# Sums of the weights of the last stages made early and kept in DRAM, and rows of x added by transfers

## The chip, the core and the metric

The kernel runs on one core of a Trainium2 chip. The metric is device time in microseconds (us) of one execution; the time before is the median of three runs. A core has five engines with one instruction queue each, and they meet only through semaphores: TensorE (PE, with its weight loads as PEld), VectorE (DVE), ScalarE (ACT), GpSimd (POOL) and SyncE (SP). In this kernel SP and POOL issue the DMA transfers. An engine takes its instructions strictly in order, so one that waits holds back everything behind it.

## The reference

x is 1024 tokens by 1024 channels, in float32. One block is computed:

```
h = rms_norm(x, norm_g);  proj = h @ w_in            # u, g_rnn, q, k, v, g_attn, m_rnn, m_attn
y_rnn  = rg_lru(conv(u)) * silu(g_rnn)               # a recurrence along the tokens
y_attn = sliding_window_attention(q, k, v) * silu(g_attn)
merged = sigmoid(m_rnn) * (y_rnn @ w_rnn_out) + sigmoid(m_attn) * (y_attn @ w_attn_out)
out = rms_norm(x + merged @ w_o, final_norm_g)
```

## The kernel before

**Products.** Every large matrix product is done by a scheme with seven block products in place of eight. A unit takes 256 output channels. Its weights are four blocks A11, A12, A21, A22 (128 partitions by 512), its right side is four block rows B11, B12, B21, B22 of four tiles each. The scheme multiplies A11 by B11, A12 by B21, A22 by T4, and the sums S1 = A21 + A22, S2 = S1 - A11, S3 = A11 - A21, S4 = A12 - S2 by T1, T2, T3 and B22, where T1 to T4 are differences of the B blocks. Each factor is cut into a high and a low part (names ending in h and l): ACT makes the high one by a cast (L430), DVE the low one by a subtraction (L431). Each block product is then three matmuls per tile (L510 to L512), so a unit is 7 x 4 x 3 = 84 matmuls.

**Stages.** After the norm of x and its transposes come 24 units of the input projection (two more are done directly, at the start): ug (recurrence branch and its gate, followed by `lru` on DVE and ACT), k, v, q, ga (attention gate), mr and ma (merge gates). Between them stand 32 attention units a00 to a37. Then come eight units for the two output projections: zr0 to zr3 on y_rnn, and za0 to za3 on y_attn. Their results are multiplied by the merge gates (tile tz, L1034). The zr results stay in SBUF as MG, and the za results are added to them, which gives `merged`. Last is the product with w_o (matmuls L1162 to L1164, PSUM tiles named o): the four blocks of MG are the A side, split into mh and ml, and w_o the B side. Its first product is A11 by B11, its second S1 by T1. From the seven products come u2, u3 and c1, to which rows of x are added on DVE, and then the norm of each row tile (`row_out`, L1182) and the store.

**Where the weights come from.** The A blocks are loaded by POOL (L421) into a class of buffers named raw; the table TUNE gives it 5 buffers. The sums S1 to S4 are made on DVE (L438) just before they are split, for the z units too. For w_o the differences T1 to T4 are made on DVE in `comb_from`.

**What sets the order.** The program first lists all operations with their reads and writes. `Plan.run` then places them one by one on the engines, by its own costs, by a priority for each operation and by the numbers in TUNE (caps of buffer classes, priorities, and `orders`, the sequence of units). That placement becomes the instruction order of each queue. So every number in TUNE can move instructions anywhere in the program; an operation with no early inputs missing may be placed far ahead of where `orders` names it.

## Time and profile before

| | |
|---|---|
| median of 3 runs (lowest to highest) | 896.63 us (896.55 to 897.25) |
| the profiled execution's own time | 896.38 us |
| its span in the profile | 894.5 us |
| PE busy | 862.4 us, 96% of the span |
| DVE busy | 772.0 us, 86% |
| ACT busy | 633.0 us, 71% |
| moved by DMA | 129.77 MB, mean 145 GB/s |

The span starts with the first instruction and ends with the last; the profiled execution's own time has 1.9 us more around it. PE is the engine to look at, since its work cannot be spread to others; wherever PE waits, the profile names the instruction that released it. Stages can be told apart by time: the first unit's products start at 47.3 us, its last evicted block is added at 91.2 us, the z units run from 653 to 805.3 us, the product with w_o from 805.3 to 886.1 us, and what follows is the end of the last rows.

### The profile page before, as it was taken

Reading aid. Unit: us, or ns where it says so; the run is one execution under the profiler, and the core shown is the slowest. Engines: PE = TensorE matmul, PEld = TensorE weight load, DVE = VectorE, ACT = ScalarE, POOL = GpSimd, SP = SyncE. Lnnn points to the kernel's source line nnn. Section 1 sums busy time; section 2 is a strip of 40 time slices with the busy share of each in tenths; the row PEclk is TensorE's granted clock in tenths of the full one; section 3 lists DMA queues with packets and bytes.
Section 4 is the critical chain, followed back from the end, with each engine's and each line's share of the span. In section 5 each row is a group of like instructions: output and inputs, shape, how many; then the busy total and the mean of one; then the engine's idle time right before and its main releaser. Section 6 shows DMA issues by size and latency. Waiting matters only on the chain.

```text
span 894.5 us, 13047 instructions
## 1 busy us (share of the span) xinstructions
PE 862.4 (96%) x4040; PEld 711.5 (80%) x4040; DVE 772.0 (86%) x1571; ACT 633.0 (71%) x1326; POOL 73.0 (8%) x131
## 2 busy tenths in 40 slices
PE   4999999999999999999999999999999989998996
PEld 3778888888777788887888887888888878877885
DVE  6995778799999858888787977677999899999998
ACT  7654485889999558786998999979874445344631
POOL 2100000000010100001001000000100100000000
PEclk9999999999999999999999999999999999999998
DMA  9314626112236675677524645353765570493005
GB/s 321 122 42 130 159 83 206 53 34 73 77 86 175 214 209 148 166 195 212 160 77 119 193 113 165 119 168 114 219 199 177 182 253 24 164 317 119 0 1 212
DMA packets 86886, 129.77 MB, mean 145 GB/s; under 512 B 10656, under 2 KB 40224, under 8 KB 86816
## 3 DMA queue, kind: packets, MB, share of 16 engines
q1 hardware_dynamic: 77216, 97.47, 35.1%
q0 software_dynamic: 9600, 31.46, 12.2%
q8 instruction: 32, 0.52, 0.2%
q14 instruction: 38, 0.31, 0.1%
HBM read 87.21 MB, written 41.68 MB: 144 GB/s over the span
## 4 chain that ended last, share of the span: by engine, by line
PE 62%; DVE 24%; ACT 8%; issue 4%; DMA 2%; SPq 0%; DVEq 0%; ACTq 0%
PE pair L510 17%; PE pair L511 16%; PE pair L512 16%; PE ps_s L901 3%; DVE cu L731 2%; PE ptp L935 2%; DVE hs L764 2%; DVE wl L431 2%; ACT sm L916 2%; DVE ml L431 2%; DVE S L438 2%; DVE c L438 1%; ACT sm L924 1%; PE fd L568 1%; PE fd L567 1%
## 5 line engine op out<-in xcount | busy, mean ns | idle before, releaser
L421 POOL DMA_DIRECT2D A<-in_wall_dram x120 | 64.6, 539 | 681.9 <-PE po L949 111.5
L430 ACT CAST wh<-S 128x512 fp32r<-128x512 f32 x128 | 78.6, 620 | 18.7 <-PE pair L512 7.8
L431 DVE TENSOR_TENSOR wl<-S,wh 128x512 fp32r<-128x512 f32 x128 | 87.0, 683 | 5.3 <-ACT wh L430 4.1
L431 DVE TENSOR_TENSOR wl<-A,wh 128x512 fp32r<-128x512 f32 x96 | 65.5, 683 | 4.7 <-ACT wh L430 3.1
L430 ACT CAST wh<-A 128x512 fp32r<-128x512 f32 x96 | 59.4, 619 | 7.6 <-PE pair L511 2.8
L916 ACT ACTIVATE sm<-sm,nm 128x256 f32<-128x256 f32 (+1 forms) x128 | 62.0, 488 | 1.0 <-DVE nm L909 0.9
L909 DVE CUSTOM_DVE_ANT_0 sm<-ps_s,mask_t,sink_t 128x256 f32<-128x256 f32 (+1 forms) x128 | 54.0, 459 | 3.4 <-PE ps_s L901 3.1
L924 ACT ACTIVATE sm<-sm,dn 128x256 f32<-128x256 f32 (+1 forms) x128 | 53.5, 489 | 2.5 <-DVE dn L921 2.4
L510 PE MATMUL pair<-T3h,wh 128*128 128x512 f32 x128 | 50.5, 395 | 1.3 <-ACT u L526 1.3
L510 PE MATMUL pair<-B11h,wh 128*128 128x512 f32 x128 | 51.2, 400 | 0.5 <-DVE B12l L427 0.5
L510 PE MATMUL pair<-T4h,wh 128*128 128x512 f32 x128 | 50.9, 397 | 0.8 <-ACT u L533 0.7
L511 PE MATMUL pair<-T2l,wh 128*128 128x512 f32 x128 | 50.0, 391 | 1.6 <-DVE T2l L431 1.6
L510 PE MATMUL pair<-T2h,wh 128*128 128x512 f32 x128 | 51.4, 401 | 0.2 <-ACT c L523 0.2
L438 DVE TENSOR_TENSOR c<-pair,u 128x512 f32<-128x512 f32 x64 | 43.8, 684 | 8.8 <-ACT u L533 4.6
L510 PE MATMUL pair<-T1h,wh 128*128 128x512 f32 x128 | 51.3, 401 | 0.0
L512 PE MATMUL pair<-B11h,wl 128*128 128x512 f32 x128 | 50.1, 391 | 1.0 <-DVE wl L431 1.0
L510 PE MATMUL pair<-B22h,wh 128*128 128x512 f32 x128 | 49.9, 390 | 0.7 <-DVE c L438 0.7
L510 PE MATMUL pair<-B21h,wh 128*128 128x512 f32 x128 | 50.6, 395 | 0.0
L512 PE MATMUL pair<-T4h,wl 128*128 128x512 f32 x128 | 50.0, 390 | 0.0
L511 PE MATMUL pair<-T3l,wh 128*128 128x512 f32 x128 | 50.0, 390 | 0.0
L512 PE MATMUL pair<-T2h,wl 128*128 128x512 f32 x128 | 50.0, 390 | 0.0
L511 PE MATMUL pair<-B22l,wh 128*128 128x512 f32 x128 | 49.9, 390 | 0.0
(270 smaller groups left out, 2588.7 us busy)
## 6 DMA issues: line engine op xcount, KB each, us to landing
A<-in_wall_dram POOLq DMA_DIRECT2D x120, 256.0 KB, 3.3
qt<-st_q SPq DMA_DIRECT2D x32, 256.0 KB, 3.9
xt<-in_x_dram SPq DMA_DIRECT2D x16, 256.0 KB, 5.4
A<-in_wall_dram SPq DMA_DIRECT2D x16, 256.0 KB, 4.9
tm_r<-tm SPq DMA_DIRECT2D x16, 256.0 KB, 2.5
K<-st_k SPq DMA_DIRECT2D x32, 128.0 KB, 3.1
yr_dr<-tg SPq DMA_DIRECT2D x16, 256.0 KB, 2.2
st_q<-qh SPq DMA_DIRECT2D x32, 128.0 KB, 2.5
```

Source lines behind the costliest of these rows:

```text
L421: pl.op([("POOL", 1000.0)], reads, writes, lambda e: nc.gpsimd.dma_start(dst(), src()), prio, move=move)
L430: ACT(lambda e: e.copy(h(), src()), cols, reads, wh, prio)
L431: (DVE if psum else EW)(lambda e: e.tensor_tensor(l(), src(), h().bitcast(F32), op=ALU.subtract), cols, list(reads) + list(wh), wl, prio)
L438: (eng or EW)(lambda e: e.tensor_tensor(dst.t, a.t, b.t, op=op), HF, [a, b], [dst], prio)
L510: nc.tensor.matmul(ps.t, h.t[:, w], bh.t, start=start and k == 0, stop=False, **kw)
L511: nc.tensor.matmul(ps.t, h.t[:, w], bl.t, start=False, stop=False, **kw)
L512: nc.tensor.matmul(ps.t, l.t[:, w], bh.t, start=False, stop=k == 3, **kw)
L731: DVE(lambda v, j=j, w=w, cu=cu, u=u: v.scalar_tensor_tensor(cu.t[:, j:], u.t[:, : HF - j], w(), cu.t[:, j:], op0=MUL, op1=ADD), HF, [u, c ...
L901: nc.tensor.matmul(ps.t[:, j, o0 : o0 + pw], qt.t[:, h, :], K[m, half].t[:, c0 : c0 + pw], start=m == 0, stop=m == 1)
L909: DVE(lambda v, ps=ps, j=j, h=h, s=s: v.tensor_tensor_reduce(s.t[:, j, :], ps.t[:, j, :], att["mask"].t[:, 256 - w : 256], scale=-0.125, s ...
L916: ACT(lambda e, h=h, s=s, j=j: e.activation(s.t[:, j, :], s.t[:, j, :], AF.Exp, scale=-1.0, bias=nm.t[:, h : h + 1], accum_out=dn.t[:, h : ...
L924: ACT(lambda e, h=h, s=s, j=j: e.activation(s.t[:, j, :], s.t[:, j, :], AF.Identity, scale=dn.t[:, h : h + 1]), w, [(s, j), dn], [(s, j)], ...
```

## The change

1. **Sums kept in DRAM.** A new function `sums(j)` loads the four blocks of a z unit again through a small buffer class sr (issued by SP), makes S1 to S4 on DVE and stores them to a DRAM tensor. Then the z unit loads S1 to S4 (through POOL, into the raw buffers) and makes no sums; it also needs no A21. `orders` names s0, s1, s3, s4, s5, s6 (units zr0, zr1, zr3, za0, za1, za2) and s10. zr2 and za3 still make their sums in place. s10 makes T1 to T4 for one quarter of w_o, but the loads of such T tiles are only built if table 8 exists, and it does not: the four tiles of s10 are made and stored and never read.
2. **Merged part in DRAM** (`mgd` 1): the zr results are stored to DRAM (16 stores) and loaded again (tile mg, 16 loads) when the za results are added.
3. **x added by transfers** (`xacc` 1): twelve of the sixteen row tiles of x are added to u3, u2 and c1 by adding transfers, which POOL issues (`ADDTO`), in place of 12 loads on SP and 12 adds on DVE.
4. **Numbers.** Nearly all numbers in TUNE and the sequence of units are others; the raw class has 4 buffers now, for A blocks and loaded sums together.

```diff
 TUNE = {
-    'm': (29, 3, 3),
+    'm': (30, 3, 3),
...
-    'raw': 5,
-    'raws': 9,
-    'S': 5,
+    'raw': 4,
+    'raws': 10,
+    'S': 6,
...
-    'gt': -5,
+    'gt': -4,
...
+    'sump': 200,
+    'sumq': 0,
+    'sr': 5,
+    'srs': 8,
+    'xacc': 1,
+    'macc': 0,
     'lo': 0,
-    'mgd': 0,
-    'orders': 'k0 ug0 v0 ug5 ug3 ug6 ug7 ug2 ug4 q0 a00 ga0 q1 ma0 a01 a02 a03 a10 q2 a11 a04 a12 q3 '
-              'ma1 a13 a05 a14 a06 a07 a15 ug1 a20 a21 mr2 ga1 a16 a17 a22 a23 a24 a25 ga3 a26 a30 '
-              'a31 a32 ga2 ma3 a33 a34 a35 a36 a27 mr3 a37 ma2 zr0 zr1 zr2 zr3 za0 za1 za2 za3',
+    'mgd': 1,
+    'orders': 'ug0 k0 ug7 v0 ug5 ug4 ug3 ug1 q0 q1 ug2 a00 ga0 ma2 a01 a02 a03 a10 a11 a04 a05 q3 a12 '
+              'a13 ga3 a14 q2 a15 s0 a06 s5 a07 s10 ug6 s3 ma1 mr3 a16 a20 a21 a17 s4 s6 a22 a23 a24 '
+              'ma0 ga2 a25 s1 a26 a30 a31 a32 a33 a34 ma3 a35 a36 a27 mr2 ga1 a37 zr0 zr1 zr2 zr3 za0 '
+              'za1 za2 za3',
...
+    def ADDTO(dst, src, nbytes, reads, writes, prio=0):
+
+        pl.op([("POOL", 1000.0)], list(reads) + list(writes), writes, lambda e: nc.gpsimd.dma_start(dst(), src(), accum_op=ADD),
+              prio, move=2 * nbytes / 16 / 2048 * 84)
...
+            if j in sum_dr:
+                if name not in A:
+                    t, m = buf(self.cls, name=name), int(name[1]) - 1
+                    A[name] = t
+                    DMA(lambda: t.t, lambda: sum_dr[j][m], 1 << 18, [(sum_dr[j], m)], [t], self.prio, by=self.by)
+                return A[name]
...
+    def sums(j):
...
+        d = sum_dr[j] = dr.tile([4, P, HF], F32, name=f"sum{j}")
+        T = {}
+
+        def raw(n, ap):
+            T[n] = load("sr", "sr")
+            DMA(lambda: T[n].t, ap, 1 << 18, [], [T[n]], TUNE["sump"], by="POOL" if TUNE["sumq"] else "SP")
+
+        def make(m, n, a, b, op):
+            t = T[n] = buf("ss", name=n)
+            tt(t, T[a], T[b], op, TUNE["sump"])
+            DMA(lambda: d[m], lambda: t.t, 1 << 18, [t], [(d, m)], TUNE["sump"])
...
+                   {n: [((lambda m=m, k=k: sum_dr[8 + k][m]), [(sum_dr[8 + k], m)]) for k in range(4)]
+                    for m, n in enumerate(("T1", "T2", "T3", "T4")) if 8 in sum_dr})
...
+    def plus_x(t, r, c):
+
+        if TUNE["xacc"]:
+            ADDTO(lambda: t.t, lambda: x[r * P : (r + 1) * P, HALF[c]], 1 << 18, [], [t], TUNE["xof"])
+            return t
+        y = x_rows(r, c)
+        tt(y, y, t, ADD)
+        return y
...
     for i in range(4):
-        XO[i + 4, 1] = x_rows(i + 4, 1)
         tt(u3[i], d[i], u3[i], ADD, 0, DVE)
-        tt(XO[i + 4, 1], XO[i + 4, 1], u3[i], ADD)
+        XO[i + 4, 1] = plus_x(u3[i], i + 4, 1)
```

How the change moves instructions is shown at three places. The first is DVE in the first 45 us, between the splits of the first unit and T1, the first difference of the second half of x. Before, the four sums there belong to a unit that soon runs:

```order
L431 TENSOR_TENSOR wl_537<-S3_497,wh_530 128x512
L703 TENSOR_SCALAR acc_95<-acc_95 128x8
L704 TENSOR_TENSOR acc_95<-acc_95,zz_255 128x8
L706 SCALAR_TENSOR_TENSOR acc_95<-acc_95,ab_126 128x8
L707 TENSOR_SCALAR sp4_547<-acc_95 128x8
L708 TENSOR_SCALAR nsp8_549<-acc_95 128x8
L438 TENSOR_TENSOR S1_554<-A21_499,A22_501 128x512
L438 TENSOR_TENSOR S2_559<-S1_554,A11_267 128x512
L438 TENSOR_TENSOR S3_564<-A11_267,A21_499 128x512
L438 TENSOR_TENSOR S4_568<-A12_528,S2_559 128x512
L668 SCALAR_TENSOR_TENSOR T1_590<-pt_573,vec_t_99,F11_292 128x512
```

And now they are five of the sums that will be kept (their inputs are sr):

```order
L443 TENSOR_TENSOR wl_565<-S3_516,wh_556 128x512
L725 TENSOR_TENSOR acc_102<-acc_102,zz_262 128x8
L450 TENSOR_TENSOR S2_573<-S1_546,sr_288 128x512
L727 SCALAR_TENSOR_TENSOR acc_102<-acc_102,ab_133 128x8
L450 TENSOR_TENSOR S3_579<-sr_288,sr_274 128x512
L728 TENSOR_SCALAR sp4_589<-acc_102 128x8
L729 TENSOR_SCALAR nsp8_591<-acc_102 128x8
L450 TENSOR_TENSOR S4_594<-sr_293,S2_573 128x512
L450 TENSOR_TENSOR S1_611<-sr_299,sr_548 128x512
L689 SCALAR_TENSOR_TENSOR T1_625<-pt_601,vec_t_106,F11_307 128x512
```

The sums of the next unit moved behind the T splits, and the kept sums begin here. All 28 of them stand in DVE's order ahead of the end of the third unit's recurrence work (the last, S4_1535, stands beside the first operations of the second `lru`), so they are made before any attention unit, not where `orders` names them.

The second place is POOL's queue at the start of the zr units. Before it holds only A blocks:

```order
L421 DMA A11_7148<-in_wall_dram 128x512
L421 DMA A21_7210<-in_wall_dram 128x512
L421 DMA A22_7280<-in_wall_dram 128x512
L421 DMA A12_7422<-in_wall_dram 128x512
L421 DMA A11_7505<-in_wall_dram 128x512
```

Now each unit that has kept sums loads seven tiles (sum0 belongs to zr0):

```order
L428 DMA A11_7069<-in_wall_dram 128x512
L428 DMA S1_7122<-sum0_93 128x512
L428 DMA S2_7255<-sum0_93 128x512
L428 DMA A12_7329<-in_wall_dram 128x512
L428 DMA S3_7393<-sum0_93 128x512
L428 DMA A22_7441<-in_wall_dram 128x512
L428 DMA S4_7474<-sum0_93 128x512
L428 DMA A11_7533<-in_wall_dram 128x512
```

Four loads in a unit became seven, through four buffers in place of five.

The third place is DVE where the last z unit ends and the product with w_o begins. ml is the low part of a block of MG, and the product A11 by B11 needs four of them. Before, three (ml_9128, ml_9135, ml_9142) stand 13 operations further ahead, and the fourth, ml_9210, behind the gate work of the last unit (c12_9166 is its last block):

```order
L1034 SCALAR_TENSOR_TENSOR tz_9178<-tz_9178,c12_9166 128x512
L438 TENSOR_TENSOR tz_8283<-tz_8283,tz_9178 128x512
L1034 SCALAR_TENSOR_TENSOR tz_9189<-tz_9189,pair_8849 128x512
L438 TENSOR_TENSOR tz_8289<-tz_8289,tz_9189 128x512
L1034 SCALAR_TENSOR_TENSOR tz_9196<-tz_9196,c22_9084 128x512
L438 TENSOR_TENSOR tz_8294<-tz_8294,tz_9196 128x512
L431 TENSOR_TENSOR ml_9210<-tz_8010,mh_9144 128x512
L438 TENSOR_TENSOR S1_9212<-tz_7863,tz_8161 128x512
```

Now the last two of the four, ml_9257 and ml_9266, stand ahead of it, with S1's first tile right behind them:

```order
L450 TENSOR_TENSOR mg_9184<-mg_9184,tz_9178 128x512
L443 TENSOR_TENSOR ml_9257<-mg_8670,mh_9242 128x512
L443 TENSOR_TENSOR ml_9266<-mg_8690,mh_9259 128x512
L450 TENSOR_TENSOR c22_9268<-pair_9119,u3_9261 128x512
L443 TENSOR_TENSOR T1l_9274<-T1_9065,T1h_9237 128x512
L450 TENSOR_TENSOR S1_9281<-mg_8564,mg_9184 128x512
```

The split that the first w_o product waits for moved from behind 13 operations to ahead of them. On PE, nine matmuls of that product now stand before the last two block products of za3, and the other 39 after them.

More of the change, by code (lines that the diff above doesn't have):

```diff
@@ L36 @@
     'pen': 99999,
-    'zy': 7,
-    'zg': 2,
-    'raw': 5,
-    'raws': 9,
-    'S': 5,
+    'zy': 5,
+    'zg': 3,
+    'raw': 4,
+    'raws': 10,
+    'S': 6,
     'wc': 11,
     'B': 11,
-    'psw': 92,
-    'psk': 0,
-    'Y': 10,
-    'ld': 9,
-    'lds': 25,
+    'psw': 58,
+    'psk': 1,
+    'Y': 9,
+    'ld': 14,
+    'lds': 21,
     'kv': 8,
-    'kvs': 4,
+    'kvs': 3,
     'qt': 3,
-    'qts': 3,
-    'P': 17,
+    'qts': 5,
+    'P': 16,
     'AO': 22,
-    'AOs': 18,
+    'AOs': 17,
     'xo': 24,
-    'lru0': -183,
+    'lru0': -135,
     'xos': 10,
-    'prep': 244,
+    'prep': 270,
     'att': 91,
     'val': 95,
-    'gate': 893,
-    'lru': -1188,
-    'qk': -306,
-    'comb': 349,
-    'ztl': 300,
-    'xof': 497,
-    'gzr': 14,
-    'gza': 44,
+    'gate': 951,
+    'lru': -1407,
+    'qk': -125,
+    'comb': 348,
+    'ztl': -10,
+    'xof': 233,
+    'gzr': 8,
+    'gza': 42,
     'gwo': 14,
     'gxo': 3,
-    'gt': -5,
+    'gt': -4,
     'seven': 'ra',
@@ L484, in left @@
                 return raw(name)
+            j = self.i - U_ZR if self.i < U_K else 4 + self.i - U_ZA
+            if self.i not in range(U_ZR, U_K) and self.i < U_ZA:
+                j = -1
+            if j in sum_dr:
[4 more added lines that the diff above has]
+                return A[name]
             src = A[name] = buf("S", name=name)
@@ L992, in whole_from, with comb_from @@
         return get
-    def comb_from(src, after, prio):
+    def comb_from(src, after, prio, more={}):
         C, Y, T = {}, {}, {}
@@ L1008, in right @@
                 return raw(n)
+            if n not in T and n in more:
+                T[n] = [load("Y", n) for _ in range(4)]
+                for k in range(4):
+                    DMA(lambda k=k: T[n][k].t, more[n][k][0], 1 << 18, more[n][k][1] + after, [T[n][k]], prio)
             if n not in T:
@@ L1076, in hybrid_block_kernel @@
     for w in TUNE["orders"].split():
[L1077 removed]
+        seq.append(("a", int(w[1]), int(w[2])) if w[0] == "a" else ("s", int(w[1:])) if w[0] == "s" else (w[:-1], int(w[-1])))
     base = {"ug": U_UG, "mr": U_MR, "k": U_K, "v": U_V, "q": U_Q, "ma": U_MA, "ga": U_GA, "zr": U_ZR, "za": U_ZA}
[L1079 removed]
+    ids = [base[a] + p for a, p in (it for it in seq if len(it) == 2 and it[0] != "s")]
     POS.update({u: i for i, u in enumerate(ids)})
@@ L1123, in hybrid_block_kernel @@
     for it in seq:
+        if it[0] == "s":
+            sums(it[1])
+            continue
         if len(it) == 2:
@@ L1222, in hybrid_block_kernel @@
     for i in range(4):
-        tt(XO[i, 0], b[i], c1[i], ADD, 0, DVE)
+        tt(XO[i, 0], b[i], XO[i, 0], ADD, 0, DVE)
         row_out(i, [XO[i, 0], XO[i, 1]])
```

35 lines of the change are left out of this document (26 added, 9 removed).

## The prediction

> **What bounds the kernel now.** I read the engine table first, then the busy time by stage, then the waits of PE, then the timeline at the longest late wait.
>
> ```profile
> PE 862.4 (96%) x4040; PEld 711.5 (80%) x4040; DVE 772.0 (86%) x1571; ACT 633.0 (71%) x1326; POOL 73.0 (8%) x131
> ```
>
> The change touches no matmul, so PE's work stays and only its 894.5 - 862.4 = 32.1 us without work, and time at a lower clock, can go. Where they lie is in the table of stretches (columns: stretch in us and its length; busy us and instructions of PE, PEld, DVE, ACT, POOL; granted clock, DMA share, GB/s). The stretches are the start, the first unit, units with VectorE free, units with VectorE full, attention, the z units, the first product with w_o, its other six, and the end. The last two rows, from a second table, are the two z units in which PE waits.
>
> ```profile
> 7.90:47.30 39.40, 33.81 (x161) 27.25 (x161) 36.18 (x97) 29.99 (x64) 8.32 (x6) 0.96 0.60 215
> 47.30:91.20 43.90, 43.56 (x191) 35.71 (x192) 33.44 (x54) 20.38 (x38) 2.69 (x5) 1.00 0.32 86
> 91.20:186.00 94.80, 94.80 (x427) 78.20 (x426) 74.77 (x127) 64.99 (x109) 8.05 (x15) 1.00 0.41 122
> 186.00:281.00 95.00, 93.36 (x408) 75.93 (x408) 93.35 (x151) 88.14 (x138) 9.67 (x18) 1.00 0.26 77
> 281.00:653.00 372.00, 369.19 (x1870) 308.47 (x1870) 299.67 (x735) 315.17 (x765) 32.24 (x60) 1.00 0.58 165
> 653.00:805.30 152.30, 149.07 (x654) 121.98 (x654) 148.28 (x244) 73.30 (x134) 11.28 (x21) 1.00 0.55 184
> 805.30:820.20 14.90, 12.66 (x48) 9.65 (x47) 14.59 (x25) 3.83 (x9) 0.00 (x0) 0.90 0.49 172
> 820.20:886.10 65.90, 65.89 (x290) 54.20 (x288) 64.98 (x124) 32.20 (x65) 0.00 (x0) 1.00 0.14 49
> 886.10:894.50 8.40, 0.00 (x0) 0.00 (x0) 4.70 (x12) 0.59 (x2) 0.00 (x0) 0.66 0.51 187
> ...
> 729.00:748.00 19.00, 16.44 (x71) 12.84 (x70) 19.00 (x33) 10.63 (x20) 1.87 (x4) 1.00 0.16 53
> 786.00:805.30 19.30, 18.62 (x83) 15.09 (x82) 19.08 (x32) 9.41 (x18) 0.00 (x0) 1.00 0.91 321
> ```
>
> Three things are to be seen. From 653 us on VectorE is as full as PE (148.28 of 152.3 us, then 14.59 of 14.9), and here PE waits: 19.00 - 16.44 = 2.56 us in the first za unit, 19.30 - 18.62 = 0.68 in the last. From 186 to 281 us VectorE is full too (93.35 of 95), and PE loses 1.64. From 47.3 to 186 us VectorE is free for 43.90 - 33.44 + 94.80 - 74.77 = 30.5 us. The waits name VectorE:
>
> ```profile
> PE o L1164 <- DVE ml L431: 2.2, 2, 2.1
> PE pair L511 <- DVE T2l L431: 1.6, 1, 1.6
> ```
>
> The longer wait costs more than its 2.07 us. PE there (start, length in us):
>
> ```profile
> 805.29 0.39 PE L1162 MATMUL o<-B11h,mh 128*128 128x512 f32 x1
> ...
> 814.18 0.39 PE L1163 MATMUL o<-B11l,mh 128*128 128x512 f32 x1
> 816.64 0.50 PE L1164 MATMUL o<-B11h,ml 128*128 128x512 f32 x1 [2.07 <-DVE ml L431]
> ...
> 818.09 0.63 PE L1162 MATMUL o<-B11h,mh 128*128 128x512 f32 x1
> 818.52 0.63 PE L1163 MATMUL o<-B11l,mh 128*128 128x512 f32 x1
> ...
> 820.62 0.39 PE L1162 MATMUL o<-T1h,mh 128*128 128x512 f32 x1
> ```
>
> The 48 matmuls of this product take 820.62 - 805.29 = 15.33 us. At the pitch of the rest (65.89 us for 290, 0.227 each) they need 10.90, so **4.4 us** are lost: 14.90 - 12.66 = 2.2 waiting and 2.2 because matmuls after the wait start 0.43 us apart (818.52 - 818.09), at half the pace. VectorE, meanwhile:
>
> ```profile
> 805.34 1.88 DVE L431 TENSOR_TENSOR ml<-tz,mh 128x512 fp32r<-128x512 f32 x3
> ...
> 815.29 0.69 DVE L438 TENSOR_TENSOR tz<-tz 128x512 f32<-128x512 f32 x1
> 815.90 0.68 DVE L431 TENSOR_TENSOR ml<-tz,mh 128x512 fp32r<-128x512 f32 x1
> 816.50 2.49 DVE L438 TENSOR_TENSOR S<-tz 128x512 f32<-128x512 f32 x4
> ```
>
> It makes three of the four low parts, then all gate work of the last unit, then the fourth. Four adds in 2.49 us, the last 0.69 long, are 0.60 apart: one VectorE operation costs its queue 0.60 us.
>
> The Trainium skill (TensorE: Matmul & The Clock Gate, What's actually happening) has the clock halved after about 3.4 us of idleness. Here a wait of 2.07 us was enough and the half pace then lasted some 3.5 us, so the trace does not bear out that length. By the page this product would lose only the 2.2 us.
>
> **The change part by part.** *Sums out of the z units.* Their prices on VectorE, and those of the adds of x:
>
> ```profile
> L438 DVE TENSOR_TENSOR S<-A,A 128x512 f32<-128x512 f32 x64 | 43.6, 682 | 0.8 <-PE pair L511 0.8
> L438 DVE TENSOR_TENSOR xo<-xo,u 128x512 f32<-128x512 f32 x8 | 5.5, 693 | 0.3
> ```
>
> Six units lose four sums each: 24 x 0.60 = 14.4 us off VectorE after 653 us. Part of that is refilled, since splits of the right sides come later in the order. Counting VectorE's instructions between the last blocks (c12) of successive units, times 0.60 us, the eight units hold 31, 11.5, 14.5, 19, 27, 11.5, 20.5, 21 us before and 30.5, 12, 15.5, 18.5, 23, 13, 14, 19 now, against 19 us of PE each. Summing what exceeds 19 and working off what falls short, VectorE arrives at w_o about 4 us behind before and level with PE now; at the first za unit it is 8 behind before and 4.5 now. What remains of the 2.56 + 0.68 us lies between nothing (at zr0 both orders put VectorE some 12 us behind and PE did not wait) and all of it; I take 0.5, as the new lag is the smaller one. **Term: -2.7.**
>
> *First product with w_o.* The fourth split is now ahead of the last gate work, and behind the end of za3 PE has 39 matmuls, 8.9 us, before it needs the low part of S1. From c12_9329 to that split are 11 operations, 6.6 us, so it is ready some 2 us early; the next three follow 1.2 us apart against a need every 0.68 us, and the last is just in time. The next narrow place is T3l, queued behind 14 other splits: counted on at 0.60 us it comes 0.5 to 1 us after PE asks. I leave 1.0 of the 4.4 (bounds: 0, and 4.4 if a wait of 2 us forms again). **Term: -3.4.**
>
> *Sums put in early.* 28 sums x 0.60 = 16.8 us on VectorE before 186 us, in the 30.5 us that it has free; four of them (s10) serve nothing, which costs 2.4 us only if the cover is gone. Ahead of T1 stand five sums where there were four.
>
> ```profile
> 44.85 0.75 DVE L668 SCALAR_TENSOR_TENSOR T<-pt,vec_t,F 128x512 f32<-128x512 f32 x1 [0.51 <-ACT B12h L426]
> ```
>
> T1 waited 0.51 us for ACT, so the fifth sum costs between 0 and 0.6; sr loads on SP stand between the stores of the gates and are issued some 2 us before use. **Term: +0.4.** Counted as above, the second unit now holds 24 us of VectorE work, so it falls up to 5 us behind PE there, less than the 7 that the units from 186 to 281 us added up to before, at a loss of 1.64. There the recurrence units no longer run in one row (q0, q1 between), so I take half of that back. **Term: -0.8** (bounds +1 and -1.6).
>
> *Merged part through DRAM.* 32 more transfers on SP and no VectorE work; the zr stores end a unit before their loads. In the same stage 12 loads of x leave. Late transfers show as VectorE waiting for tz, 1.1 us at most before; loads may now start one product (2.7 us) earlier. **Term: 0** (bounds +2, if each late tile waits as the worst one did, and -1).
>
> *x by adding transfers.* 12 adds x 0.60 = 7.2 us off VectorE after 805 us, where PE did not wait past 820.6: nothing to win there but the last row.
>
> ```profile
> 846.00 0.68 DVE L438 TENSOR_TENSOR u<-o,u 128x512 f32<-128x512 f32 x1
> ...
> 865.47 0.68 DVE L438 TENSOR_TENSOR u<-o,u 128x512 f32<-128x512 f32 x1
> ...
> 886.41 0.68 DVE L438 TENSOR_TENSOR xo<-o,c 128x512 f32<-128x512 f32 x1
> ```
>
> The last add starts 0.31 us after the last matmul (886.10); a freer VectorE can give that back. **Term: -0.3.** No adding transfer is in the trace. Nearest rows:
>
> ```profile
> A<-in_wall_dram POOLq DMA_DIRECT2D x120, 256.0 KB, 3.3
> xo<-in_x_dram SPq DMA_DIRECT2D x16, 256.0 KB, 5.8
> L421 POOL DMA_DIRECT2D A<-in_wall_dram x24: 536/538/545, 642.1 to 774.6; - x24
> DMA to landing us min/median/max: 2.8/3.1/6.9
> ```
>
> Below it costs one POOL load, 3.1 us; above, twice an x load under traffic, 11.6 us, as it also reads its target. I take 6. The last u2 is made at 866 us and wanted at about 884, so even 11.6 us hides. POOL has nothing queued behind these twelve.
>
> *Attention, 281 to 653 us.* Its order is new throughout, and PE lost 2.81 us of 372 there; one recurrence unit more falls into it, while ACT and VectorE keep 57 and 72 us free. **Term: 0** (bounds -2 and +3).
>
> Sum: -2.7 - 3.4 + 0.4 - 0.8 - 0.3 = -6.8. The profiled execution's own time was 896.38 (span 894.5 and 1.9 around it), so 889.6; the median of the runs shown lies 0.25 above it: **889.8 us**.
>
> **Rivals.**
>
> *A, half the gain.* VectorE still meets 23 us of work against 19 in the first za unit, so the 2.56 us stay, or T3l waits 2 us and the half pace follows. For it: the page shows how a wait of 2.07 cost 4.4. Against it: the counts. Time: 889.8 + about 3.5 = 893.3.
>
> *B, taken back.* Early sums stand between links of the first recurrence units, and attention in its new order loses time: with the upper bounds of the start (0.2 more), the early units (1.8) and attention (3) and half that of the merged part (1), 889.8 + 6.0 = 895.8, no difference. For it: VectorE has hardly a gap from 47 to 130 us. Against it: PE had 100% there and the units hold work ahead.
>
> *C, slower, by the feed of weights.* Seven loads in a unit go through four raw buffers, so a buffer must turn round in 4 x 19 / 7 = 10.9 us (23.8 before, with five buffers and four loads). A turn is the issue 0.54, the landing, the cast and the subtraction, and the time these wait in their queues.
>
> ```profile
> L430 ACT CAST wh<-A 128x512 fp32r<-128x512 f32 x96 | 59.4, 619 | 7.6 <-PE pair L511 2.8 <-DVE tz L1034 2.4 <-DMA A<-in_wall_dram 1.8
> L431 DVE TENSOR_TENSOR wl<-A,wh 128x512 fp32r<-128x512 f32 x96 | 65.5, 683 | 4.7 <-ACT wh L430 3.1
> ```
>
> With 3.1 to land that is 4.9 us, and 6 are left for queueing; with 6.9 it is 8.7, and 2.2 are left. From 10.9 us on, PE waits. At 12.4, 1.5 x 7 / 4 = 2.6 us a unit, six units are 16 us: 889.8 + 16 = 906. Against it: the median landing, and that casts and subtractions of these tiles have one place each in the order.
>
> *D, slower, by the adding transfers.* If the eight on u3 and u2 run one after the other at T each from 846 us, the last is done at 846 + 8T, wanted at 884: it decides from T = 4.8. At 8 us the end moves by 26 us, to about 916. Against it: x loads were issued 0.4 us apart and overlapped.
>
> ```profile
> 797.51 4.43 SPq L419 DMA_DIRECT2D xo<-in_x_dram  x6
> ```
>
> A rule speaks for D. The Trainium skill (DMA: Bandwidth & Descriptors, SWDGE vs HWDGE vs iDMA) says that descriptors which GpSimd writes can be held up by VectorE. POOL's issues here took 536 to 545 ns with VectorE 97% busy, so the trace shows nothing of it.
>
> *E, the sums are not where the change says.* True by the order: they stand at the start, not among the attention units. It does not alter the sum, as the room was counted there, and so has no chance of its own.
>
> **How the numbers follow.** Forecast 0.57, A 0.21, B 0.10, C 0.08, D 0.04. The time is that of the forecast, 889.8. Its own range, from the bounds that move singly, is 886 to 893.5; for 8 in 10 the range must reach A and most of B: 885.5 to 896.5. A measurement of this kernel can tell 0.2%, 1.8 us, from no change. Faster by more than that, below 894.8: the forecast and A, 0.78. Within: B and a little of A, 0.10. Slower: C and D, 0.12.
>
> **What would show it.** In the profile after: from 653 us on VectorE visibly below PE, no wait of PE for ml at the first w_o product, and that product with granted clock 1.00; the first za unit with PE over 18.5 of 19 us; 47 to 186 us with VectorE above 120 of 138.7 us and PE still full; PE's waits for T3l at or under 1 us. Wrong would be waits of PE or ACT for loaded S tiles (C), ACT's squares waiting for u (D), or new waits of more than 2 us before 653 us (B).

## The result, and the profile after

The changed kernel takes **885.48 us** (median of four runs, 885.22 to 885.57); the kernel before takes 896.59 (four runs, 895.72 to 897.25). The ratio is 0.9876, with a 95% interval of 0.9859 to 0.9893: 11.1 us gained, where 6.8 were forecast. The time lies 0.02 us under the low end of the range, 885.5, less than the runs differ among themselves. On another chip the changed kernel took 885.40 us (884.20 to 885.76).

The profiled execution took 885.57 us, with a span of 883.8. The engine table of the page after:

```profile
PE 860.1 (97%) x4040; PEld 710.7 (80%) x4040; DVE 764.6 (87%) x1555; ACT 640.1 (72%) x1339; POOL 93.3 (11%) x161
```

PE still makes 4040 matmuls, and is busy 2.3 us less: 862.4 before, part of it at half pace. What it does not work fell from 32.1 to 883.8 - 860.1 = 23.7 us. Where, the stretches tell (the table of stretches of the kernel after, columns as in the prediction; the stretches are those of before, except that the last two meet where the last matmul now ends):

```profile
7.90:47.30 39.40, 34.10 (x160) 27.74 (x160) 36.72 (x99) 30.16 (x64) 7.72 (x5) 1.00 0.77 271
47.30:91.20 43.90, 43.55 (x192) 36.09 (x193) 41.55 (x68) 20.98 (x38) 2.37 (x4) 1.00 0.61 206
91.20:186.00 94.80, 93.97 (x419) 76.36 (x419) 85.27 (x146) 66.52 (x114) 8.58 (x16) 1.00 0.61 197
186.00:281.00 95.00, 94.67 (x415) 77.29 (x414) 86.70 (x138) 78.00 (x123) 9.67 (x18) 1.00 0.32 100
281.00:653.00 372.00, 371.49 (x1883) 311.47 (x1883) 304.30 (x743) 329.64 (x782) 33.87 (x63) 1.00 0.56 165
653.00:805.30 152.30, 151.91 (x670) 124.43 (x669) 141.47 (x230) 71.66 (x133) 20.78 (x38) 1.00 0.75 251
805.30:820.20 14.90, 14.78 (x65) 11.92 (x65) 14.83 (x26) 8.25 (x16) 2.62 (x3) 1.00 0.40 69
820.20:875.80 55.60, 55.59 (x245) 45.40 (x243) 47.72 (x92) 30.09 (x64) 7.00 (x8) 1.00 0.42 104
875.80:883.80 8.00, 0.00 (x0) 0.00 (x0) 4.52 (x12) 0.59 (x2) 0.00 (x0) 0.78 0.53 197
```

From 653 to 805 us VectorE is now visibly below PE (141.47 of 152.30 us; 148.28 before); in the next stretch it is still full (14.83 of 14.90). PE loses 0.39 us in the first of these, 0.12 in the second and 0.01 after it. Attention lost 2.81 us before and loses 0.51 now. From 91 to 186 us, where PE lost nothing, it now loses 0.83. The waits of PE over the whole run, longest first (what waited and for what: us in total, times, longest):

```profile
PE pt L656 <- DVE xt L649: 9.0, 2, 8.3
PE fd L588 <- DVE B11l L439: 1.5, 1, 1.5
PE fd L589 <- DVE B21l L439: 1.2, 1, 1.2
PE fd L589 <- DVE B11l L439: 1.2, 1, 1.2
PE pair L531 <- DVE B12l L439: 0.6, 1, 0.6
```

All five lie in the first 48 us. The waits for ml, T2l and wl, which were the longest behind 653 us before, are gone, and none for T3l came in their place. The transfers that are new or changed (tile, queue, count, size, median us from issue to landing):

```profile
S<-sum POOLq DMA_DIRECT2D x24, 256.0 KB, 4.5
...
tz<-tm_r SPq DMA_DIRECT2D x16, 256.0 KB, 7.2
...
u<-in_x_dram POOLq DMA_DIRECT2D x8, 256.0 KB, 4.6
```

An adding transfer lands in 4.6 us (the eight on u3 and u2, in this row) or 4.2 (the four on c1), nearer to its lower bound than the 6 that were taken. The gate tiles tz now need 7.2 us, 3.1 before. That is not, in the main, the merged part: in the twelfth experiment, which keeps that part in SBUF, they still need 6.6, and in the third, with the new order alone, 4.2.

### The profile page after: what moved, and what is told of

Its sections match the earlier page's. It is cut to its first block, busy times and chain, and to the rows that moved or that the text cites. A ratio compares the mean times of both kernels' runs of the same rounds, so it can differ in the third digit from the quotient of the medians.

```text
span 883.8 us, 13278 instructions
## 1 busy us (share of the span) xinstructions
PE 860.1 (97%) x4040; PEld 710.7 (80%) x4040; DVE 764.6 (87%) x1555; ACT 640.1 (72%) x1339; POOL 93.3 (11%) x161
## 4 chain that ended last, share of the span: by engine, by line
PE 58%; DVE 17%; ACT 6%; DMA 4%; issue 3%; DVEq 0%; SPq 0%; ACTq 0%
PE pair L531 15%; PE pair L532 15%; PE pair L533 15%; PE ps_s L922 3%; PE ptp L956 2%; DVE wl L443 2%; PE o L1233 2%; PE o L1232 2%; PE o L1231 2%; DVE c L450 1%; DVE S L450 1%; ACT sm L945 1%; PE po L969 1%; DVE cu L752 1%; PE po L970 1%
## 5 line engine op out<-in xcount | busy, mean ns | idle before, releaser
L428 POOL DMA_DIRECT2D A<-in_wall_dram x114 | 61.5, 540 | 591.1 <-PE pair L533 128.1
L532 PE MATMUL pair<-T4l,wh 128*128 128x512 f32 x128 | 50.0, 391 | 0.1
L532 PE MATMUL pair<-B11l,wh 128*128 128x512 f32 x128 | 50.0, 390 | 0.0
L532 PE MATMUL pair<-T1l,wh 128*128 128x512 f32 x128 | 49.9, 390 | 0.0
```

Of the source, the lines that this page charges most:

```text
L428: pl.op([("POOL", 1000.0)], reads, writes, lambda e: nc.gpsimd.dma_start(dst(), src()), prio, move=move)
L532: nc.tensor.matmul(ps.t, h.t[:, w], bl.t, start=False, stop=False, **kw)
```

## The experiments

In most of these kernels the order is kept: the planner runs on the unchanged list of operations, and its result is edited before the instructions are issued, so that every instruction that is not named stands where it stood. Where the planner had to run anew, the text says so. Times are medians. Each ratio is to the kernel before, timed beside it (896.6 to 897.3 us). The changed kernel itself was timed beside experiments 10 to 12 only (experiment 9: 885.40 us, ratio 0.9866, 0.9850 to 0.9882); the distances to it that are given for the others are those of medians, over chips too. The start, up to 47 us, varies from run to run: in the profiles of kernels that have the same instructions there, PE was busy between 32.81 and 35.23 us from 7.9 to 47.3. Differences under about 1 us are therefore read from the stretch they belong to, not from the total.

### 1 and 5: the sums' time put back on VectorE

```diff
+            ops.append(dict(fn=lambda e, b=b, nc=self.nc: nc.vector.tensor_tensor(b.t, b.t, b.t, op=ALU.max), deps=(), note="again", bufs=[b]))
+            seq.insert(k, (0.0, len(ops) - 1, "DVE"))
```

> The changed kernel with every instruction in its place, and one VectorE operation more on each of the 24 kept sums that the z units load: the maximum of the tile with itself, ahead of its cast. It has the form of the sum that stood there before (128x512, two SBUF reads) and changes no value. Only VectorE's work after 653 us comes back, 24 x 0.60 = 14.4 us; the loads, the orders and the early sums stay. Theory 1 (VectorE's load in the z units and its lag at w_o cost what the prediction's terms 1 and 2 say): PE waits again in the za units and at the products with w_o, and the end moves by 3 to 6 us, to 888.5-891.5. Rival (the new order of the planner took the waits away and would carry the sums as well): VectorE's own gaps after 653 us, some 10 us, take most of it and the end moves by less than 1 us, to under 886.5.

Measured: **906.84 us** (ratio to before 1.0114, 1.0098 to 1.0131), 21 us above the changed kernel, far more than either expected. The longest wait of ACT from 650 to 806 us in this kernel (S L344 is the added operation):

```profile
ACT wh L458 <- DVE S L344: 49.3, 19, 4.8
```

The added operation stood directly ahead of its cast. VectorE's queue is behind there, so ACT waited 49.3 us for it, and VectorE then waited 6.2 us for such casts. Most of the price was that chain, not the 14.4 us of work, as the fifth experiment confirms. Here k is the place of that cast. In the fifth experiment it is another:

```diff
+            k = [q for q in range(k) if seq[q][2] == "DVE"][-4]
...
             seq.insert(k, (0.0, len(ops) - 1, "DVE"))
```

> As the first experiment, with each of the 24 added VectorE operations four places earlier in VectorE's queue (2.4 us), so that the cast on ACT finds its tile ready, as it did where sums were made well ahead. In the first experiment ACT waited 49.3 us for these operations and VectorE 6.2 us for the casts behind them. Theory 1 (the price is VectorE's time: 14.4 us against some 10.5 us that VectorE has free from 650 to 793 us): the end moves by 3 to 7 us, to 888.5-892.5. Rival (the price is the longer chain from the load over VectorE to the cast, wherever the operation stands): the end stays above 900 us.

Measured: **893.24 us** (ratio 0.9960, 0.9948 to 0.9972), 7.8 us above the changed kernel. The stretches:

```profile
653.00:805.30 152.30, 145.04 (x630) 116.25 (x629) 145.52 (x239) 73.04 (x133) 19.83 (x37) 1.00 0.72 241
805.30:820.20 14.90, 14.31 (x64) 11.47 (x62) 14.20 (x24) 4.75 (x9) 2.65 (x3) 1.00 0.60 150
```

PE loses 152.30 - 145.04 = 7.26 us in the z units (0.39 without the added work) and 0.59 in the next stretch. So the rival of experiment 5, the chain wherever it stands, falls: 13.6 us between two kernels with the same work lie in four places of a queue. But the chain is shorter, not gone:

```profile
ACT wh L460 <- DVE S L344: 22.1, 12, 3.7
```

The 7.8 us are therefore what the sums cost on VectorE at these places, and an upper bound for its time alone.

### 2: one split moved in the kernel before

```diff
         lo = on("DVE", "lo")
+        behind(lo[3], max(list(ops[lo[3]]["deps"]) + lo[2:3], key=[x[1] for x in seq].index))
```

> The kernel before with one instruction moved: the fourth split of the first product with w_o (815.90 us on VectorE) stands right behind the third, ahead of the last gate work. All else is in its place. Theory A (the prediction's term 2: 2.2 us of waiting and 2.2 at half pace hang on this one split): the end moves by up to 4.4 us, to 892.2. Theory B (the wait was only the first face of VectorE's lag): PE comes to the second product some 4 us earlier, but the four sums S behind the gate work begin at 816.5 as before, and their low parts are ready at 819.6, 820.8, 822.0 as before; PE waits for those and the end moves by 1 us at most, to 895.6 or more.

Measured: **896.03 us** (ratio 0.9995, 0.9984 to 1.0007): no difference. The waits of PE at the product with w_o in this kernel (start, length, instruction, wait and what ended it):

```profile
804.74 0.50 PE L1189 MATMUL o<-B11h,ml 128*128 128x512 f32 x1 [0.68 <-DVE ml L454]
816.40 0.50 PE L1187 MATMUL o<-T1h,mh 128*128 128x512 f32 x1 [0.91 <-ACT mh L453]
818.10 0.50 PE L1189 MATMUL o<-T1h,ml 128*128 128x512 f32 x1 [0.97 <-DVE ml L454]
```

The wait of 2.07 us and the half pace behind it are gone, and PE now waits for S1, whose sums stand behind the gate work as before. From its first matmul of the product to its last, PE needs 1.0 us less than before (79.8 for 80.8). The last rows take it back: before, the last add on VectorE began 0.31 us after the last matmul ended; here that matmul ends at 883.2 us, and the add begins 1.6 us later.

```profile
884.85 0.68 DVE L461 TENSOR_TENSOR xo<-o,c 128x512 f32<-128x512 f32 x1
```

Theory B holds: the 4.4 us did not hang on one split, but on VectorE's lag, of which that split was the first face.

### 3 and 4: the three new things apart from the new order

In experiment 3 the planner runs anew, with the new numbers and sequence but without the three things:

```diff
-    'xacc': 1,
-    'mgd': 1,
-    'orders': '... a15 s0 a06 s5 a07 s10 ug6 s3 ...
+    'xacc': 0,
+    'mgd': 0,
+    'orders': '... a15 a06 a07 ug6 ...
```

> The changed kernel with the new numbers of the planner and the new order of the units, but without the three new things: no kept sums, x added on VectorE, merged part in SBUF. The planner sets the order anew. Theory 1 (the three things carry the gain): 892 to 897 us, with VectorE as full as PE after 653 us and PE waiting there as in the kernel before. Rival (the new order of the units carries it): the waits in attention, 2.3 us, stay away and the end comes at 888 us or under.

Measured: **898.35 us** (ratio 1.0017, 1.0007 to 1.0027). The total is near theory 1, 1.4 us above its range. The stretches show more (the last ends with the last matmul):

```profile
186.00:281.00 95.00, 94.75 (x417) 77.74 (x416) 87.66 (x141) 77.65 (x122) 9.92 (x19) 1.00 0.34 104
281.00:653.00 372.00, 371.06 (x1875) 309.90 (x1874) 305.07 (x743) 327.39 (x779) 31.90 (x60) 1.00 0.55 162
653.00:805.30 152.30, 148.38 (x642) 119.89 (x641) 147.02 (x241) 73.40 (x133) 11.80 (x22) 0.99 0.53 180
805.30:820.20 14.90, 14.31 (x62) 11.16 (x61) 14.73 (x25) 4.16 (x9) 0.00 (x0) 1.00 0.39 140
820.20:885.70 65.50, 62.71 (x274) 50.92 (x273) 64.52 (x125) 28.23 (x54) 0.00 (x0) 1.00 0.12 43
```

Up to 653 us the new order alone has the gain: 0.25 us lost from 186 to 281 (1.64 before) and 0.94 in attention (2.81 before). After 653 us it has nothing: 3.92 + 0.59 + 2.79 = 7.3 us lost, and the last rows take 10.3 us (8.4 before, 8.0 in the changed kernel), as VectorE comes late to them. So the order brought the gain in attention and among the recurrence units. The gain behind 653 us needs the three things, in an order that was planned for them.

Experiment 4 is the other half: the three things with the old numbers and sequence, planned anew (the cut is against the kernel before).

```diff
-    'orders': '... a00 ga0 q1 ma0 ...
+    'orders': '... a00 s0 s5 s10 s3 s4 s6 s1 ga0 q1 ma0 ...
+    'xacc': 1,
+    'mgd': 1,
```

> The counterpart: the kernel before with its own numbers and order of the units, and the three new things added: the seven sets of sums in one row behind the first attention unit (a00), x by adding transfers, merged part through DRAM. The planner sets the order anew. Theory 1 (the three things carry the gain): 888 to 892 us, with the waits of attention as before (2.5 us) and those after 653 us gone. Rival (the gain is in the new order and numbers): 895 us or more.

Measured: **948.26 us** (ratio 1.0562, 1.0535 to 1.0588), 52 us slower than before. The rival had said 895 us or more, but nothing of this size. The longest waits of PE, but for the start:

```profile
PE o L1229 <- DVE T2l L440: 11.2, 1, 11.2
...
PE psb L763 <- DVE ul L440: 8.2, 5, 6.0
```

They lie all over the program. The things alone do not carry a gain; with numbers that were not set for them, the planner's order loses far more than they bring.

### 6, 10 and 11: x added on VectorE again

```diff
+            ops.append(dict(fn=lambda e, y=y, t=t: self.nc.vector.tensor_tensor(t.t, y.t, t.t, op=ALU.add), deps=(), note=None, bufs=[y, t]))
+            seq[k] = (0.0, len(ops) - 1, "DVE")
+            ops.append(dict(fn=lambda e, y=y, r=r, c=c: self.nc.sync.dma_start(y.t, self.x(r, c)), deps=(), note=None, bufs=[y]))
+            seq.insert(k - 40, (0.0, len(ops) - 1, "SP"))
```

All twelve (6), the four on c1 (10), the eight on u3 and u2 (11), the order kept: k is the place where the adding transfer was issued, and the load stands 40 operations ahead of it.

> The changed kernel with every other instruction in its place, and the twelve adding transfers of x turned back into loads on SP and adds on VectorE, each add where the transfer was issued. Theory 1 (the prediction's term 5: VectorE has room after the first product with w_o, nothing to win but in the last row): the end moves by 0 to 0.5 us, under 886. Rival (the four adds on c1 stand among the splits of the second to fourth product, where VectorE is full): 2.4 us more ahead of T2l and T3l, PE waits there, and at half pace behind it: 887 to 890 us.

> As the sixth experiment, but only the four adds on c1 are back on VectorE; the eight on u3 and u2 stay adding transfers. Theory P (it is the place: two of the four stand ahead of the low parts of S1, for which PE waited 0.69 and 0.84 us in the sixth experiment): 1.5 us above the unchanged kernel. Rival (VectorE's time, wherever it is spent): a third of what twelve cost, 1.3 us at most, and no wait for the low parts of S1.

> The other part: only the eight adds on u3 and u2 are back on VectorE, from about 840 us on. Theory P (the place): no wait of PE, 0 to 0.5 us above the unchanged kernel, and that in the last rows. Rival (VectorE's time): two thirds of what twelve cost, 2.5 us above it.

Measured: **889.31 us** with all twelve (ratio 0.9924, 0.9906 to 0.9942), **888.42** with the first four (0.9904, 0.9888 to 0.9920) and **885.60** with the last eight (0.9872, 0.9854 to 0.9891), beside 885.40 for the changed kernel itself:

> The changed kernel itself, timed again beside the runs of this call, which are read against it: 885 to 887 us if the chip is as the first one. In the profile the wait of PE for the first scaled rows of x and the first wait for a low part of the first right side show how much the start varies by itself (8.3 and 1.45 us in the first profile).

PE in the tenth kernel, its waits behind 786 us:

```profile
811.27 0.50 PE L1249 MATMUL o<-T1h,ml 128*128 128x512 f32 x1 [0.63 <-DVE ml L459]
813.08 0.51 PE L1249 MATMUL o<-T1h,ml 128*128 128x512 f32 x1 [0.84 <-DVE ml L459]
```

And the same place in the changed kernel, first VectorE, then PE (two answers):

```profile
807.33 1.89 DVE L450 TENSOR_TENSOR S<-mg 128x512 f32<-128x512 f32 x3
809.14 0.68 DVE L443 TENSOR_TENSOR ml<-S,mh 128x512 fp32r<-128x512 f32 x1
```

```profile
810.12 0.39 PE L1233 MATMUL o<-T1h,ml 128*128 128x512 f32 x1
```

The first low part of S1 is ready at 809.14 + 0.68 = 809.82, and PE asks for it at 810.12: 0.3 us to spare (in the profile of experiment 9, the same kernel, PE waits 0.24 us there). Two of the four adds on c1 stand ahead of that low part, 1.2 us of VectorE, and the third between it and the next: those are the two waits. The last eight show no cost: 0.2 us by medians, and no new wait of PE. Theory P, the place, holds; its size does not, since 3.0 us were lost by medians and the two waits make 1.5. Experiment 6 came where its rival said, 889 us, but by these same two waits (0.69 and 0.84 us) and not by T2l and T3l.

### 7: the early sums left out

```diff
+        return [q for q in seq if not str(self.ops[q[1]]["note"]).startswith("s")]
...
-                    DMA(lambda: t.t, lambda: sum_dr[j][m], 1 << 18, [(sum_dr[j], m)], [t], self.prio, by=self.by)
+                    DMA(lambda: t.t, lambda: wall[self.i, m], 1 << 18, [(sum_dr[j], m)], [t], self.prio, by=self.by)
...
+            pl.note = f"s{it[1]}"
             sums(it[1])
```

> The changed kernel with every other instruction in its place, without the 28 sums before 186 us and their 28 loads and 28 stores; the z units load blocks of the weights in place of the kept sums, so the products of these units are not the reference's. It shows what making the sums costs. Theory 1 (the prediction's term 3: 0.4 us at the start, VectorE's free time covers the rest): 885 us, 0.3 to 0.6 us less than with them. Rival (they also delay the first recurrence units: PE lost 0.83 us from 91 to 186 us, nothing there before): 883.5 to 884.5 us.

Measured: **883.70 us** (ratio 0.9861, 0.9846 to 0.9875), 1.7 us less by medians than with the sums; the two intervals overlap (0.9850 to 0.9882 with them), so the total alone does not settle it. The stretches do better:

```profile
47.30:91.20 43.90, 43.90 (x195) 36.28 (x194) 34.32 (x57) 20.74 (x38) 2.91 (x5) 1.00 0.22 67
91.20:186.00 94.80, 94.80 (x426) 78.07 (x425) 79.89 (x135) 68.61 (x118) 8.04 (x15) 1.00 0.49 136
```

The 0.83 us that PE lost from 91 to 186 us come back (experiments 5, 6, 9, 10 and 11, with the same instructions there, lose 0.83 to 1.2). In the changed kernel they were two waits, 0.43 us for a copy u on ACT and 0.40 for an operation c of the recurrence on VectorE. The 0.35 us of the stretch ahead do not count: they are the wait for B12l at 47.66 us, which falls ahead of 47.3 in other profiles. So the rival holds in kind: the early sums are paid by delays from 91 to 186 us, though VectorE has 9.5 us free there with them. About 0.8 us of that price is shown; whether it is more stays open.

### 8 and 14: a better version

```diff
+        seq = [q for q in seq if ops[q[1]]["note"] != "s10"]
...
+        for k, i in enumerate(sm):
+            behind(i, rest[k])
```

> A try at a better version: the changed kernel without the four sums that nothing reads (s10, with four loads and four stores), and with the 28 small operations of 128x8 that make the constants of the recurrence moved from the start (20.8 to 43.8 us on VectorE, some 5 us) to single places behind the splits of T4, some 60 us in. All else is in its place. Theory 1 (at the start VectorE's queue is what PE waits for): PE's waits of 1.16 and 1.22 us for the low parts of the first right side go, T comes as much earlier, and the end comes at 883 us. Rival (VectorE is full to 186 us, so what is moved is paid there): within 0.5 us of 885.5.

Measured: **883.81 us** (ratio 0.9856, 0.9840 to 0.9872). That lies between the two theories, and its interval overlaps that of the changed kernel. The first unit's products began at 45.33 us (47.20 in the ninth experiment), but the first product with w_o at 793.25 (792.80 there): the gain was gone by then. Of PE's waits at the start the 1.2 us for B21l is gone, the 2.6 us for B11l are not; and one of 1.19 us for another B21l came in the first za unit. The waits of VectorE from 700 to 750 us:

```profile
DVE tz L1093 <- DMA tz<-tm_r: 3.4, 3, 1.8
```

Experiment 14 adds a change in SP's queue: three loads of tz ahead of four loads of YB.

```diff
+        for i in reversed(y):
+            behind(i, z)
```

> The eighth kernel (start freed of small operations, no dead sums) with three SP loads of tz from tm_r moved ahead of the four loads of YB from ya_dr at 708 us. In the eighth kernel VectorE waited 1.8, 0.9 and 0.7 us for such tz at 719 to 724 us, and PE 1.2 us for B21l behind them, so that the 1.9 us won at the start were gone by 793 us. Theory (the queue's order is the cause, the DMA engines have room): these waits go and 1 to 1.5 us stay won: 882.5 us. Rival (from 715 to 745 us the DMA engines are full, 383 to 397 GB/s, and what is moved ahead is paid behind): as the eighth kernel, 883.8 us, with VectorE waiting for YB in its place.

Measured: **882.88 us** (882.18 to 884.92; ratio 0.9843, 0.9830 to 0.9857). The waits of VectorE in the same window:

```profile
DVE tz L1103 <- DMA tz<-tm_r: 1.6, 2, 1.4
DVE YB L485 <- DMA YB<-ya_dr: 1.4, 3, 0.9
```

The wait for tz is halved and half of what was won goes to YB, and PE's wait of 1.2 us for B21l is gone. So both theories hold in part (from 715 to 745 us the DMA engines are indeed full in the eighth kernel, a share of 1.00, but at 349 GB/s). By medians this version is 2.5 us faster than the changed kernel, on another chip; the interval of its ratio still touches that of the changed kernel (0.9850 to 0.9882). Its profiled execution, the slowest of its five, shows no gain: the first product with w_o begins at 793.30 us, and PE has a new wait of 0.90 us in attention. So that it is better is likely at most, not proven.

### 12 and 13: the merged part in SBUF

```diff
-    'mgd': 1,
+    'mgd': 0,
```

> The changed kernel with the merged part kept in SBUF, as before; sums and x stay as changed, and the planner sets the order anew around the 16 tiles that are then held through the eight z units. Theory 1 (the prediction's term 4, nothing gained or lost by the way through DRAM itself): within 1.5 us of the unchanged kernel. Rival (the 16 tiles that it frees are what lets the kept sums be loaded ahead of their use): 4 us above it or more, with waits of PE or ACT for loaded tiles in the za units.

Measured: **913.15 us** (ratio 1.0186, 1.0164 to 1.0208). The time fits the rival, its reason only in small part. ACT does wait for loaded A blocks in the z units, 8.3 us in three waits where the changed kernel has none, and PE loses 2.2 us in that stretch (0.39 in the changed kernel). But nearly all of the 27.7 us to the changed kernel is one wait in the product with w_o, and not for a loaded tile:

```profile
PE o L1232 <- DVE B11l L443: 23.9, 1, 23.9
```

The planner had put six splits of w_o's right side behind some 60 other operations on VectorE (the expectation below says 30). Moved forward, the rest kept:

```diff
         for k in (2, 3):
+            behind(b[1][k], b[1][k - 1])
+            behind(b[0][k], b[0][k - 1])
...
```

> The twelfth kernel (merged part in SBUF), order kept, with six splits moved: the last two of B11 and the four of T1 for the products with w_o, which the planner had put behind 30 other operations on VectorE (829 to 833 us; PE waited 23.9 us for the first of them), now stand behind the first two of B11, at about 792 us. Theory R (room: with 16 tiles held by the merged part there is no tile for them before the sums S give some back): the moved splits wait for tiles where they stand, and the end stays above 905 us. Rival (an accident of the planner's order; the tiles are there): the wait of 23.9 us goes, T2l waits some 5 us in its place, and the end comes at 892 to 898 us.

Measured: **898.47 us** (ratio 1.0016, 1.0005 to 1.0028): 14.7 us come back, just outside what the rival said. The moved splits ran from 790 to 794 us without a wait: the tiles were there, and theory R falls. The next such place is a copy on ACT:

```profile
PE o L1265 <- ACT c L1274: 6.1, 1, 6.1
```

What a planner that was set for it would lose with the merged part in SBUF stays open. That the way through DRAM is worth 27.7 us is not shown.

### 15: a wait of attention in the kernel before

```diff
         u = on("ACT", "u2")[15]
+        behind(act[act.index(u) - 1], u)
```

> The kernel before with two neighbours on ACT changed over, in attention: the copy u that frees a bank of PSUM (412.1 us) goes ahead of a cast wh that waited 5 us for PE to free its tile (411.5 us); PE waited 1.32 us for this copy. Theory (what attention lost, 2.8 us, were such single accidents of order, and a new order wins them without the three new things): the end moves by 1.3 us, to about 895.3. Rival (work held back there is only met again later, VectorE being full from 653 us): no change, 896.6.

Measured: **895.63 us** (ratio 0.9990, 0.9981 to 0.9999), 1.05 us less by medians (0.1 to 1.7 by the interval). ACT before, then in this kernel, and what PE waits for the copy in both:

```profile
411.48 0.62 ACT L430 CAST wh<-S 128x512 fp32r<-128x512 f32 x1 [4.97 <-PE pair L512]
412.12 0.59 ACT L526 COPY u<-pair 128x512 f32<-128x512 f32 x1
```

```profile
410.58 0.59 ACT L551 COPY u<-pair 128x512 f32<-128x512 f32 x1 [4.98 <-PE pair L536]
```

```profile
412.76 0.50 PE L510 MATMUL pair<-T3h,wh 128*128 128x512 f32 x1 [1.32 <-ACT u L526]
```

```profile
411.22 0.50 PE L534 MATMUL pair<-T3h,wh 128*128 128x512 f32 x1 [0.68 <-ACT u L551]
```

The copy stood behind a cast that waited for PE, and PE waited for the copy. With the two changed over PE waits 0.64 us less; the rest of its wait is the copy itself (0.59 us), which can begin only when PE has finished the tile. The theory holds in kind, with half of the wait won at that place; whether all of it stays won to the end is within the noise.

## Why the prediction came out 4.3 us too high

By its own steps, in the profiled executions (in all 896.38 - 885.57 = 10.8 us):

| Step | forecast | measured | from |
|---|---|---|---|
| sums out of the z units | -2.7 | -2.8 | 3.23 us lost before, 0.39 after |
| first product with w_o | -3.4 | -4.3 | 4.4 before, 0.13 after |
| sums put in early, start to 47.3 us | +0.4 | -0.3 | 5.59 before, 5.30 after; it varies by more than that |
| the same, 47.3 to 186 us | 0 | +0.8 | 0.34 before, 1.18 after |
| the same, 186 to 281 us | -0.8 | -1.3 | 1.64 before, 0.33 after |
| merged part through DRAM | 0 | not visible | PE loses 0.39 us in all of the z units |
| x by adding transfers | -0.3 | -0.4 at the tail, more ahead of it | 8.4 to 8.0; experiments 6, 10, 11 |
| attention | 0 | -2.3 | 2.81 before (1.96 in experiment 2), 0.51 after |
| sum | -6.8 | -10.6 | |

**Right: what carries the gain behind 653 us.** VectorE was the bound there, and taking sums off it moved the end. The first two terms said 6.1 us, the profile has 7.1, and experiment 5, which puts the same work back, 7.8. It bears out the sum of the two terms, not how they divide it: there PE loses 7.26 us in the z units and 0.59 in the stretch behind them. The counting of VectorE's work per unit against 19 us of PE was enough for the sum.

**The step that failed: attention put at 0.** It makes 2.3 of the 4 us. The prediction said that the order there was new throughout and that 2.81 us were lost, and took a value near the middle of its bounds, -2 and +3. But the two sides were not alike: the 2.81 us were waits of the old order and could go; for a loss it gave no reason, with ACT and VectorE having 57 and 72 us free. The runs showed 0.51 us lost in its place. Experiment 3 has 0.94 from the new order alone, so 1.9 of the 2.3 us, and experiment 15 shows one such accident, two neighbours on ACT. Why the other waits went was not tried. The bound of -2 was also too tight, as all of 2.81 could go. How much the old order lost varies: experiment 2 has the same instructions up to the last product, and there a wait of 0.74 us for a block c (303.3 us) is missing and attention loses 1.96. So the term is 1.5 to 2.3 us, still the largest of the misses.

**Mis-sized: the product with w_o.** 1.0 us was left for a wait for T3l that did not come; 0.13 us are lost. The reason given for the 4.4 us was too narrow. It was not that the split stood behind the gate work (experiment 2: moved, it brings nothing), but that VectorE came late to everything there. That the term came out near is partly luck: the adds on c1, which are no longer in the way (below), were not counted in it.

**Wrong in place: x by adding transfers.** The prediction saw "nothing to win there but the last row", because PE did not wait past 820.6 us before. But three of the twelve adds would stand ahead of or among the low parts of S1 in the new order, where 0.3 us are to spare; experiment 10, with all four on c1, costs 3.0 us by medians, of which its profile shows 1.5 as waits. A part of the second term's gain is theirs. The last row itself came out as said, 8.4 to 8.0 us.

**Wrong in place: the early sums.** They were put at 0.4 us at the start, and paid 0.83 from 91 to 186 us, where the prediction saw VectorE fall up to 5 us behind and put down no loss. Experiment 7 has the whole at 1.7 us by medians, of which 0.83 are seen as waits. The loss was more than made up among the units from 186 to 281 us, and experiment 3 shows that this, too, was the order (0.25 us lost there without the sums). What the sums cost at the start cannot be told: it varies there by 2.4 us.

**Landing of the tiles.** The prediction put the merged part at 0 and had loads start earlier. They land later (tz 7.2 us for 3.1), but PE loses only 0.39 us in all of the z units, so the term stands at 0 as far as PE shows it. Experiments 12 and 13 do not isolate it, as the planner set another order there.

**The rivals.** A (half the gain): the first za unit has PE at 18.95 of 19 us (724 to 743 us). B: of its parts only the delay in the early units came. C: neither PE nor ACT waits for a loaded S tile in the four raw buffers. D: the adding transfers landed in 4.2 to 4.6 us, under the 4.8 from which it decides, and the next was issued before the last had landed. (The row that the prediction gave against D has six issues in 4.43 us, so the loads of x were some 0.7 us apart, not 0.4; they overlapped all the same.) E: as it said. Of the signs of the forecast one did not come: VectorE has 126.8 of 138.7 us from 47 to 186, as foreseen, but PE is not quite full beside it. One sign of being wrong did come, and was harmless: ACT's squares waited 6.9 us for u, in six waits, as the prediction named for D. They had waited 7.2 us for VectorE's adds before, and ACT is busy for only 30.09 of the 55.6 us there.

## What to carry to other kernels

When a change comes with a new order, the waits of the old order are themselves a term: list them, and ask which of them belong to the resource that the change frees and which are accidents of a queue. The second kind may go with the order, and nothing as large need come in its place, though experiment 4 shows that it can. And price work on a full engine by where it stands in the queue: the same 14.4 us of VectorE cost 7.8 us four places earlier and 21 directly ahead of the cast, and of twelve equal adds eight showed no cost.

## What the runs showed of the hardware

**Half pace after a wait.** Matmuls 0.43 us apart came after waits of 1.35, 1.91, 2.07, 4.8, 6.1 and 23.9 us, but not after 2.13 (third experiment) and 2.87 (fifth). So the length of one wait does not decide it, and the prediction's "how a wait of 2.07 cost 4.4" is one case and no rule. The granted clock in the traces shows more. In every profile, from its first record to the last matmul, it stays at full or at half speed for a whole multiple of 3.413 us before it changes (3.413 us at half speed before, 6.8 in the first experiment, 23.9 in the twelfth). Cut at these steps, the stretches around the wait of 2.07 us in the kernel before are the first two, and those around the wait of 2.13 us in the third experiment the last two (columns as in the prediction):

```profile
813.75:817.16 3.41, 1.34 (x6) 0.83 (x5) 3.34 (x7) 0.00 (x0) 0.00 (x0) 1.00 0.70 225
817.16:820.57 3.41, 3.41 (x9) 2.64 (x9) 3.41 (x7) 3.07 (x6) 0.00 (x0) 0.50 0.00 0
```

```profile
859.32:862.73 3.41, 2.35 (x11) 1.62 (x9) 3.34 (x7) 2.21 (x5) 0.00 (x0) 1.00 0.00 0
862.73:866.14 3.41, 2.34 (x10) 1.94 (x11) 3.34 (x8) 2.37 (x4) 0.00 (x0) 1.00 0.00 0
```

The wait of 2.07 us lies whole in one step, in which PE is busy for 1.34 us, and the next step runs at half clock (0.50). The wait of 2.13 us falls across two steps, PE is busy for 2.3 us in each, and the clock stays at 1.00. So it counts where a wait falls as well as how long it is. A sharp limit is not shown: 1.35 us with 0.29 more in the same step was enough in the third experiment, 1.74 us in one step of the fourth was not. The Trainium skill (TensorE: Matmul & The Clock Gate, What's actually happening) says that the chip watches a free-running window of about 3.4 us. The steps agree with that; that waits of 1.35 and 2.07 us, shorter than the window, were enough does not agree with its "after ≥1 idle window".

**Adding transfers.** POOL needs 0.87 us to issue one (median of the twelve), 0.54 for a plain load, and 256 KB land in 4.5 us (3.7 to 5.2; a plain load by POOL 3.4). Ten of the twelve were issued while VectorE was 95 to 99% busy (803 to 813 and 840 to 850 us). One of these took 1.22 us, the second of two that were issued one right behind the other; the others took 0.87 to 0.90, so VectorE's work shows no delay of them.

**The order is chaotic in its numbers.** The same three things cost 52 us with one set of planner's numbers and bring 13 with another (948.26 against 896.6, 885.4 against 898.35). One copy in the wrong place cost PE 0.64 us (experiment 15), six splits 23.9 (experiment 12).
